# Queue order in the down products and the first attention blocks of a two-layer hybrid trunk: matmul-bound kernel, one core

## The chip, the core and the metric

The kernel runs on one core of a Trainium2 chip. The metric is the time of one execution in microseconds (us) on the device. A core has a matrix engine (TensorE, PE in the profile, with PEld for its weight loads), a vector engine (VectorE, DVE), an activation engine (ScalarE, ACT), a general engine (GpSimd, POOL) and a sync engine (SyncE, SP), which here only issues transfers. Each engine works through its own list of instructions in the order in which they stand there; engines wait for each other through semaphores. Matmuls write to eight PSUM banks, from which VectorE and ScalarE read.

## The reference

Two layers, on 512 tokens of 1024 features in f32. Cut to what matters:

```python
h = rms_norm(x, mix_norm[0])                      # layer 0
q, k, v, cb, cc, cx = split(h @ hy_w_in, ...)     # attention 512+128+128, convolution 3 x 512
attn = sliding_window_attention(rope(norm(q)), rope(norm(k)), v, sinks)   # window 128, blocks of 128
conv = cb * causal_conv3(cc * cx)
x = x + concat(attn, conv) @ hy_w_out
h = rms_norm(x, mix_norm[1])                      # layer 1: chunked gated linear attention
x = x + gla(h, ...) @ gla_w_out
# after the mixer of each layer i
u = causal_conv3(rms_norm(x, ffn_norm[i]) @ w_up[i]) + b[i]     # 1024 -> 2 x 2816
x = x + (gelu(u_gate) * u_up) @ w_down[i]                       # 2816 -> 1024
x = x + sigmoid(rms_norm(x, ple_norm[i]) @ w_gate[i]) * (p[i] @ w_proj[i])
```

## The kernel before

Activations are kept transposed: features on the 128 partitions, the 512 tokens along a row; `xT[0]` to `xT[7]` are the eight rows of x. Every large product is made of three matmuls in a rounded f32 format: each operand is split into a high part (ScalarE rounds it, `activation(h, src, Copy)`) and a low part (VectorE subtracts, `tensor_tensor(l, src, h, subtract)`), and high x high, high x low and low x high are summed in PSUM (`mm3`, lines 166 to 168). So each piece of weights costs one ScalarE and one VectorE instruction before PE may use it: `cut` (lines 146 and 147, tiles `wh` and `wl`), `cut_blocks` (852 and 853) and `split` (109 and 110).

PSUM is held in two pools of four banks, `ps` and `pa`. Weights arrive from memory in `raw` buffers (two), loaded through the SP queue.

Who decides the order. The program is traced top to bottom, and a planner orders each engine's instructions by priority (the order of tracing) and by when they become ready by its own estimate of times. Two things are fixed by hand: inside `manual_schedule(engines=...)` the engines named keep the order of tracing, and `with tc.issue_after(x):` puts every instruction traced in the block on x's own engine behind x in that engine's list. It adds no wait: an instruction of another engine in the block is not touched.

**Layer 0's mixer (`mixer0`).** After keys, values and the four query blocks, PE alternates between the convolution's projections ("x", "c" and "b", each in two pieces `j2` of 256 columns: `conv_in`, 48 matmuls) and the attention of four blocks t of 128 queries: `query_turned(t)` (PE transposes, ScalarE copies to `qT`, line 547), `scores(t)` (PE, line 611; VectorE adds the mask and takes row maxima, 620; then the small steps 627 to 631, the last of which is `es`; ScalarE takes the exponentials, 634), `probs(t)` (scaling, 648 and 652; PE transposes 16 tiles, 658; copies to `pT`, 664 and 666, the latter kept as `copied[t, g]`), and `mix(t)` (675). Each piece of the later convolution weights is cut in two halves, `conv_halves`, whose second half is traced later; their order is tied to copies of the attention. `conv_taps` starts with a ScalarE copy `cxs` (722). `load_vectors1` loads four small vectors through the POOL queue into rows, transposes them on PE (226) and copies them to `vec1` (227). PE's order in this part is the planner's.

**The down projection (`down`).** The product with w_down runs in units u of 256 columns, by a written plan of ordinary pieces (`cut`, 512 columns of tokens) and of block products: eight of the 22 row tiles go through a seven-product scheme on 2 x 2 blocks (`seven`, lines 905 to 907, 256 columns), one such product s for each unit, interleaved with steps of an ordinary piece. For a block product the weights are needed in forms. `first_forms` rounds two blocks as they are, and then makes two differences in place (876 and 877); `cut_blocks(ev)` rounds those (`t13`); `more_forms` makes two more. Inside `seven`, four ScalarE copies carry partial sums from bank to bank (916, 917, 926, and 930, which is `turned_over`). For s = 1 and 3 the weights come in two `zt` buffers (`load_inner`), and first_forms splits two blocks with `split`; for s = 0 and 2 they come in `raw`, and one `cut_blocks` rounds both. At the end of a block product its two sums are added to `xT` by VectorE (`add`, line 1213), which frees their banks for the next one. PE's order here is the traced one, the other engines' is the planner's.

When a row of xT is complete, `finish(m)` prepares it for the next stage: in layer 0 `advance`, in layer 1 `blocks`, which for odd m makes block sums `s12` and `s34` and splits them (`parts`).

Of the kernel before, what the change touches and what calls it, by code (L numbers as in the profile page):

```python
# [14 lines left out]
ALU = mybir.AluOpType  # L15
# [41 lines left out]
class Kernel:  # L57
# [147 lines left out]

        self.nc.gpsimd.tensor_copy(x, self.gate[: x.shape[0]])

    def columns(self, name, views, q=None):

        nc = self.nc  # L210
        n = sum(v.shape[0] for v in views)
        rows = self.sp.tile([P, P], F32, tag="vrow", name=self.nm("vrow"))
        if q is None and self.gate is not None:
            self.late(rows[:, :1])
        at = 0
        for v in views:
            (q or nc.gpsimd).dma_start(rows[at : at + v.shape[0], :], v)
            at += v.shape[0]
        if q:

            nc.scalar.copy(self.few(4, "rs", 4), self.mhalf[:, :4])
        col = self.cp.tile([P, -(-n // 64) * 64], F32, tag=name, name=self.nm(name), bufs=1)[:, :n]

        def finish():
            ps = self.pa()
            nc.tensor.transpose(ps[:, :n], rows[:n, :], self.ident[:n, :n])
            (nc.vector.tensor_copy if q else nc.scalar.copy)(col, ps[:, :n])
            return col

        return finish if q else finish()  # L230

    def load_vectors0(self):
        a = self.a
# [9 lines left out]
    def load_vectors1(self):  # L243
        a = self.a
        f = lambda v: v.rearrange("i (k p) -> (i k) p", p=P)
        v = self.columns(
            "vec1", [f(a["ffn_norm"]), f(a["ple_norm"]), f(a["hy_conv_w"][0]), f(a["gla_o_norm"])]
        )
# [42 lines left out]
    def blocks(self, m, gain, scratch, tags):  # L291


        nc = self.nc
        H = S // 2
        gx = scratch()
        nc.scalar.activation(gx, self.xT[m], AF.Copy, scale=gain[:, m : m + 1])

        def parts(x):
            w = x.shape[1]  # L300
            h, l = self.pair(self.fp, *tags)
            self.halves = self.split((h[:, :w], l[:, :w]), x)
            return lambda b, c: (h[:, b * H + c * P : b * H + (c + 1) * P], l[:, b * H + c * P : b * H + (c + 1) * P])

        if m % 2 == 0:
            self.even = gx
            self.e1 = parts(gx[:, :H])
            self.e1_split = self.halves
        else:
            e, o = self.even, gx  # L310
            op = parts(o)
            s12, s34 = scratch(), scratch()
            nc.vector.tensor_tensor(s12[:, :H], e[:, H:], o[:, H:], ALU.add)
            nc.vector.tensor_tensor(s12[:, H:], s12[:, :H], e[:, :H], ALU.subtract)
            s12p = parts(s12)
            nc.vector.tensor_tensor(s34[:, :H], e[:, :H], e[:, H:], ALU.subtract)
            nc.vector.tensor_tensor(s34[:, H:], o[:, :H], s12[:, H:], ALU.subtract)
            s34p = parts(s34)
            e1 = self.e1
            at = lambda f, b: lambda c: f(b, c)  # L320
            self.forms.append(
                dict(e1=at(e1, 0), o1=at(op, 0), o2=at(op, 1), s1=at(s12p, 0), s2=at(s12p, 1), s3=at(s34p, 0),
                     s4=at(s34p, 1))
            )
        self.squares(m)
# [101 lines left out]
    def mixer0(self):  # L427
        nc, a, tc = self.nc, self.a, self.tc
        with tc.tile_pool(name="m0", bufs=1) as mp:
# [165 lines left out]
            ss, dens, copied, mixed = {}, {}, {}, {}  # L595
            ya = [self.pair(self.fp, "b0", "b1") for _ in range(4)]

            def scores(t):

                w = 2 * P if t else P  # L600
                k0 = (t - 1) * P if t else 0
                mask = self.amask if t else self.amask[:, P:]
                s = mp.tile([P, NQ, 2 * P], F32, tag="s", name=self.nm("s"), bufs=2)
                mx = self.few(8, "mx")
                for h2 in range(2):

                    pbs = [self.pa(), self.pa()]
                    for hh in range(2):
                        hq = 2 * h2 + hh
                        for g in range(2):  # L610
                            nc.tensor.matmul(
                                pbs[g][:, hh * 256 : hh * 256 + w],
                                qTs[t][64 * g : 64 * g + 64, hq, :],
                                kT[64 * g : 64 * g + 64, k0 : k0 + w],
                                start=True, stop=True,
                            )
                    for hh in range(2):
                        for g in range(2):
                            head = 4 * g + 2 * h2 + hh
                            nc.vector.tensor_tensor_reduce(  # L620
                                s[:, head, :w], pbs[g][:, hh * 256 : hh * 256 + w], mask,
                                scale=1.0, scalar=-1e30, op0=ALU.add, op1=ALU.max,
                                accum_out=mx[:, head : head + 1],
                            )

                nm = self.few(8, "nm")
                nc.vector.scalar_tensor_tensor(out=nm, in0=mx, scalar=HD**-0.5, in1=sink, op0=ALU.mult, op1=ALU.max)
                nc.vector.tensor_scalar_mul(nm, nm, -1.0)
                den = self.few(8, "den")
                es = self.few(8, "es")  # L630
                nc.vector.tensor_tensor(es, sink, nm, ALU.add)
                nc.scalar.activation(es, es, AF.Exp)
                for head in range(NQ):
                    nc.scalar.activation(
                        s[:, head, :w], s[:, head, :w], AF.Exp, bias=nm[:, head : head + 1], scale=HD**-0.5,
                        accum_out=den[:, head : head + 1],
                    )
# [58 lines left out]
            def conv_halves(nme, j2, ins):  # L696
# [5 lines left out]
                def half(ins):  # L702
                    c = slice(len(ws) * P, len(ws) * P + P)
                    with tc.issue_after(ins):
                        ws.append(self.cut(raw[:, :, c], "b"))

                half(ins)
                return (lambda k, a, b: ws[a // P](k, 0, P)), half

            def conv_in(nme, w):  # L710
# [6 lines left out]
            def conv_taps(j2):  # L717
                for c in range(2):
                    j = 2 * j2 + c
                    xs = mp.tile([P, S], F32, tag="cxs", name=self.nm("cxs"), bufs=2)  # L720
                    pad = mp.tile([P, S + 2], F32, tag="pad", name=self.nm("pad"), bufs=2)
                    nc.scalar.copy(xs, pss["x", c])
# [19 lines left out]
                    yc[2 * j2 + c] = hl  # L742


            w = conv_w("x", 0)
            R = self.spread()
            qn0 = query(0)
# [1 line left out]
            conv_in("x", w)  # L749
            w = conv_w("c", 0)  # L750
            query_turned(0, qn0)
            self.load_vectors1()
            self.gate = None
            R2 = self.sp.tile([P, S], F32, tag="R", name="R2")
            nc.gpsimd.tensor_tensor(R2, R, R, ALU.mult)
            qn2 = query(2)
            query_turned(1, qn1)
            scores(0)
            conv_in("c", w)
            w, second = conv_halves("b", 0, copied["q", 1])  # L760
            conv_taps(0)
# [3 lines left out]
            second(copied[0, 1])  # L765
            scores(1)
            conv_in("b", w)
            w, second = conv_halves("x", 1, copied[0, 1])
            conv_out(0, (0,))
            query_turned(3, qn3)  # L770
            mix(0)
            probs(1)
            with tc.issue_after(copied[1, 0]):
                conv_out(0, (1,))
            second(mixed[0])
            scores(2)
            conv_in("x", w)
            w, second = conv_halves("c", 1, copied[1, 1])
            second(copied[1, 1])
            mix(1)  # L780
            probs(2)
            scores(3)
            conv_in("c", w)
            w, second = conv_halves("b", 1, copied[2, 1])
            second(copied[2, 1])
            conv_taps(1)
            mix(2)
            probs(3)
# [75 lines left out]
    def first_forms(self, ev, od, raw=None):  # L864
# [5 lines left out]
        else:  # L870
            h, l = self.wide("wh", 16), self.wide("wl", 48)
            h, l = (x.rearrange("p (j u n) -> p j u n", u=2, n=P) for x in (h, l))
            for u, b in enumerate((b11, b21)):
                self.split((h[:, :, u], l[:, :, u]), b)
            plain = lambda j, c: (h[:, j, c], l[:, j, c])
        nc.vector.tensor_tensor(b11, b12, b11, ALU.subtract)
        nc.vector.tensor_tensor(b12, b22, b12, ALU.subtract)  # L877
        return plain

    def more_forms(self, ev, od):  # L880
# [245 lines left out]
    def down(self, i, acts, forms, both, work, finish):  # L1126
# [93 lines left out]
        with tc.manual_schedule(engines={ET.PE}):  # L1220
# [4 lines left out]
            for t, (u, name, k0, k1, s) in enumerate(plan):  # L1225
# [34 lines left out]
                else:  # L1260
# [20 lines left out]
                    if s == 3:  # L1281
                        banks[3] = [X, Y]
                    else:
                        add(2 * s, X)
                        add(2 * s + 1, Y)
                    pend()
                    due[s] -= 1
                    block_left -= 1
# [865 lines left out]
```

## Time and profile before

| what | value |
|---|---|
| median of 3 runs | 1199.35 us (1198.14 to 1199.67) |
| the profiled execution, its own time | 1199.04 us |
| its span, first to last instruction | 1197.2 us |
| instructions | 17966 |
| granted TensorE clock | 1.000 |
| busy: DVE, ACT, POOL | 994.0, 684.0, 42.9 us |
| memory read and written | 114.37 MB and 2.10 MB, 97 GB/s over the span |
| chain that ended last, by engine | PE 89%, DVE 5%, ACT 3%, issue 2%, POOL 1% |

Busy time is the time in which an engine has an instruction on record. The views used are: the page's shares and slices; the waits (who waited for whom); the timeline (instructions in order of time, equal neighbours merged, with the idle time before them and what ended it in brackets); and the groups of instructions by line, with the busy time, the mean duration and the idle time before them. In a row, `wl<-raw,wh` names the tile written and those read, `128x1024` partitions by elements.

### The profile page before, as it was taken

The page shows a single profiled execution, that of the slowest core. Times are in us where ns is not written, and L with a number is a line of the kernel's source. Part 1 is how long each engine was busy: PE and PEld are TensorE (multiplying, and loading weights), DVE is VectorE, ACT ScalarE, POOL GpSimd, SP SyncE. Part 2 cuts the span into 40 slices and gives each one's busy share as a digit, 9 for nine tenths or more (in the row PEclk, how much of TensorE's full clock was granted, in tenths as well). Part 3 has the DMA queues.
Part 4 walks back from the last instruction along what each step waited for, and adds up shares of the span by engine and source line. Part 5 has one row for each costly group of instructions (what it writes and reads, how often), then busy time and mean ns, then how long its engine had stood idle before and what let it go on. Part 6 is the DMA issues. An engine that isn't in the chain of part 4 may idle for free.

```text
span 1197.2 us, 17966 instructions
## 1 busy us (share of the span) xinstructions
PE 1189.6 (99%) x7121; PEld 1039.0 (87%) x7121; DVE 994.0 (83%) x1571; ACT 684.0 (57%) x1116; POOL 42.9 (4%) x64
## 2 busy tenths in 40 slices
PE   9999999999999999999999999999999999999998
PEld 8877789999998888989988988889999999889887
DVE  6777687899999986789779876687999999976895
ACT  7566465655565644566563664555555656643764
POOL 2600000000000000000100000000000000000000
PEclk9999999999999999999999999999999999999999
DMA  7212322424232332232412222323242424323601
GB/s 223 85 58 72 108 71 71 142 71 141 71 122 90 122 126 97 97 106 64 148 59 70 73 70 71 106 67 110 71 141 71 141 71 131 125 89 97 212 1 71
DMA packets 110856, 117.62 MB, mean 98 GB/s; under 512 B 2824, under 2 KB 105794, under 8 KB 110772
## 3 DMA queue, kind: packets, MB, share of 16 engines
q1 hardware_dynamic: 109936, 115.88, 29.9%
q8 instruction: 56, 0.92, 0.3%
q0 software_dynamic: 560, 0.42, 0.3%
q10 hardware_dynamic: 276, 0.18, 0.1%
q14 instruction: 28, 0.23, 0.1%
HBM read 114.37 MB, written 2.10 MB: 97 GB/s over the span
## 4 chain that ended last, share of the span: by engine, by line
PE 89%; DVE 5%; ACT 3%; issue 2%; POOL 1%; DMA 0%; SPq 0%; DVEq 0%; ACTq 0%; POOLq 0%
PE ps L166 12%; PE ps L168 12%; PE ps L167 12%; PE pa L167 7%; PE pa L166 7%; PE pa L168 7%; PE ps L905 6%; PE ps L907 6%; PE ps L906 6%; PE pa L907 2%; PE pa L905 2%; PE pa L906 2%; PE ps L1519 1%; PE ps L1518 1%; PE ps L1517 1%
## 5 line engine op out<-in xcount | busy, mean ns | idle before, releaser
L146 ACT ACTIVATE wh<-raw 128x1024 fp32r<-128x1024 f32 (+4 forms) x144 | 143.4, 999 | 97.0 <-PE ps L167 59.3
L147 DVE TENSOR_TENSOR wl<-raw,wh 128x1024 fp32r<-128x1024 f32 (+4 forms) x144 | 165.7, 1151 | 28.6 <-ACT wh L146 27.7
L852 ACT ACTIVATE wh<-raw 128x1024 fp32r<-128x1024 f32 x84 | 89.3, 1063 | 121.6 <-DVE raw L877 65.4
L965 DVE SCALAR_TENSOR_TENSOR zt<-z,vfa,zt 128x510 f32<-128x510 f32 (+1 forms) x176 | 130.6, 744 | 5.3 <-ACT zt L963 4.7
L853 DVE TENSOR_TENSOR wl<-raw,wh 128x1024 fp32r<-128x1024 f32 x84 | 102.6, 1221 | 20.6 <-ACT wh L852 20.5
L963 ACT ACTIVATE zt<-z,vfb 128x512 f32<-128x512 f32 x88 | 71.0, 809 | 20.8 <-DVE four L1016 8.3
L166 PE MATMUL ps<-b,wh 128*128 128x512 f32 x192 | 76.2, 397 | 0.0
L167 PE MATMUL ps<-b,wh 128*128 128x512 f32 x192 | 75.0, 391 | 0.0
L168 PE MATMUL ps<-b,wl 128*128 128x512 f32 x192 | 74.9, 390 | 0.0
L905 PE MATMUL ps<-four,wh 128*128 128x256 f32 x256 | 71.6, 280 | 0.0
L907 PE MATMUL ps<-four,wl 128*128 128x256 f32 x256 | 71.1, 278 | 0.0
L906 PE MATMUL ps<-four,wh 128*128 128x256 f32 x256 | 70.9, 277 | 0.0
L167 PE MATMUL pa<-b,wh 128*128 128x512 f32 x176 | 69.0, 392 | 0.0
L167 PE MATMUL pa<-a,wh 128*128 128x512 f32 x176 | 69.0, 392 | 0.0
L166 PE MATMUL pa<-a,wh 128*128 128x512 f32 x176 | 69.0, 392 | 0.0
L166 PE MATMUL pa<-b,wh 128*128 128x512 f32 x176 | 69.0, 392 | 0.0
L168 PE MATMUL pa<-b,wl 128*128 128x512 f32 x176 | 68.4, 389 | 0.0
L168 PE MATMUL pa<-a,wl 128*128 128x512 f32 x176 | 68.4, 389 | 0.0
L166 PE MATMUL ps<-a,wh 128*128 128x512 f32 x128 | 50.6, 395 | 0.0
L167 PE MATMUL ps<-ul,wh 128*128 128x512 f32 x128 | 50.1, 391 | 0.0
L166 PE MATMUL ps<-uh,wh 128*128 128x512 f32 x128 | 50.1, 391 | 0.0
L167 PE MATMUL ps<-a,wh 128*128 128x512 f32 x128 | 50.0, 390 | 0.0
(496 smaller groups left out, 3591.3 us busy)
## 6 DMA issues: line engine op xcount, KB each, us to landing
raw<-in_ffn_w_up_dram SPq DMA_DIRECT2D x44, 1024.0 KB, 5.1
raw<-in_ffn_w_down_dram SPq DMA_DIRECT2D x12, 1024.0 KB, 5.2
raw<-in_hy_w_in_dram SPq DMA_DIRECT2D x8, 1024.0 KB, 5.1
raw<-in_gla_w_in_dram SPq DMA_DIRECT2D x8, 1024.0 KB, 5.1
raw<-in_ffn_w_down_dram SPq DMA_DIRECT2D x8, 768.0 KB, 4.5
raw<-in_ple_w_gate_dram SPq DMA_DIRECT2D x6, 1024.0 KB, 5.3
raw<-in_hy_w_out_dram SPq DMA_DIRECT2D x16, 256.0 KB, 4.0
zt<-in_ffn_w_down_dram SPq DMA_DIRECT2D x8, 512.0 KB, 3.6
```

The source lines that it names most:

```text
L146: nc.scalar.activation(hv, v, AF.Copy)
L147: self.rest = nc.vector.tensor_tensor(lv, v, hv.bitcast(F32), ALU.subtract)
L166: mm(out, lh, rh, start=start, stop=False, **kw)
L167: mm(out, lh, rl, start=False, stop=False, **kw)
L168: return mm(out, ll, rh, start=False, stop=stop, **kw)
L852: nc.scalar.activation(h, src, AF.Copy)
L853: nc.vector.tensor_tensor(l, src, h.bitcast(F32), ALU.subtract)
L905: mm(out, wh, xh, start=first and j == 0, stop=False, **kw)
L906: mm(out, wh, xl, start=False, stop=False, **kw)
L907: mm(out, wl, xh, start=False, stop=j == ND // 2 - 1, **kw)
L963: nc.scalar.activation(y, z, AF.Identity, scale=w2[:, f : f + 1], bias=bb[:, f : f + 1])
L965: nc.vector.scalar_tensor_tensor(out=y[:, tap:], in0=z[:, : S - tap], scalar=w[:, f : f + 1], in1=y[:, tap:], op0=ALU.mult, op1=ALU.add,)
```

## The change

Four places. (1) In the down projection `first_forms` splits the second of its two blocks after the two differences instead of before them, on VectorE behind the second difference, and the two adds of a block product to `xT` stand on VectorE behind the second difference of the next product. (2) In layer 1, for rows 0 and 1, ScalarE's rounding of s12 stands behind `turned_over`. (3) The halves of the convolution weights "x", "c" and "b" of piece 1 get further bounds: VectorE's part behind `es` of the scores then running (`begun`), and ScalarE's part of the second half of "x" behind the second `pT` copy of block 1. (4) `load_vectors1` loads earlier in the tracing and transposes after `scores(0)`; ScalarE's `cxs` copies of piece 0 stand behind the copy of query block 1.

```diff
-    def columns(self, name, views, q=None):
+    def columns(self, name, views, q=None, later=False):
...
-        return finish if q else finish()
+        return finish if q or later else finish()
...
     def load_vectors1(self):
...
+        views = [f(a["ffn_norm"]), f(a["ple_norm"]), f(a["hy_conv_w"][0]), f(a["gla_o_norm"])]
+        finish = self.columns("vec1", views, later=True)
+        def turned():
+            self.take_vectors1(finish())
+        return turned
...
     (blocks)
-            s12p = parts(s12)
+            with ExitStack() as es:
+                if m == 1:
+                    es.enter_context(self.tc.issue_after(self.turned_over.ins))
+                s12p = parts(s12)
...
     (scores)
-                nc.vector.tensor_tensor(es, sink, nm, ALU.add)
+                begun[t] = nc.vector.tensor_tensor(es, sink, nm, ALU.add).ins
...
     (conv_halves: half takes several instructions, one issue_after for each)
...
     (conv_taps)
-                    nc.scalar.copy(xs, pss["x", c])
+                    with ExitStack() as es:
+                        if not j2:
+                            es.enter_context(tc.issue_after(copied["q", 1]))
+                        nc.scalar.copy(xs, pss["x", c])
...
     (the order of mixer0)
+            vectors1 = self.load_vectors1()
             w = conv_w("x", 0)
...
             query_turned(0, qn0)
-            self.load_vectors1()
...
             scores(0)
+            vectors1()
             conv_in("c", w)
...
-            w, second = conv_halves("x", 1, copied[0, 1])
+            w, second = conv_halves("x", 1, copied[0, 1], begun[1])
...
-            second(mixed[0])
+            second(mixed[0], copied[1, 1])
...
-            w, second = conv_halves("c", 1, copied[1, 1])
-            second(copied[1, 1])
+            w, second = conv_halves("c", 1, copied[1, 1], begun[2])
+            second(copied[1, 1], begun[2])
...
-            w, second = conv_halves("b", 1, copied[2, 1])
-            second(copied[2, 1])
+            w, second = conv_halves("b", 1, copied[2, 1], begun[3])
+            second(copied[2, 1], begun[3])
...
     (first_forms)
-            for u, b in enumerate((b11, b21)):
-                self.split((h[:, :, u], l[:, :, u]), b)
+            self.split((h[:, :, 0], l[:, :, 0]), b11)
             plain = lambda j, c: (h[:, j, c], l[:, j, c])
         nc.vector.tensor_tensor(b11, b12, b11, ALU.subtract)
-        nc.vector.tensor_tensor(b12, b22, b12, ALU.subtract)
+        self.differed = nc.vector.tensor_tensor(b12, b22, b12, ALU.subtract)
+        if raw is None:
+            with self.tc.issue_after(self.differed.ins):
+                self.split((h[:, :, 1], l[:, :, 1]), b21)
...
     (down)
-                        add(2 * s, X)
-                        add(2 * s + 1, Y)
+                        with tc.issue_after(self.differed.ins):
+                            add(2 * s, X)
+                            add(2 * s + 1, Y)
```

More of the change, by code (lines that the diff above doesn't have):

```diff
@@ L245, in load_vectors1, with take_vectors1 @@
         f = lambda v: v.rearrange("i (k p) -> (i k) p", p=P)
-        v = self.columns(
-            "vec1", [f(a["ffn_norm"]), f(a["ple_norm"]), f(a["hy_conv_w"][0]), f(a["gla_o_norm"])]
-        )
+        views = [f(a["ffn_norm"]), f(a["ple_norm"]), f(a["hy_conv_w"][0]), f(a["gla_o_norm"])]
[3 more added lines that the diff above has]
+        return turned
+    def take_vectors1(self, v):
         self.g_ffn = [v[:, i * 8 : 8 + i * 8] for i in range(2)]
@@ L593, in query_turned @@
                 qTs.append(qT)
-            ss, dens, copied, mixed = {}, {}, {}, {}
+            ss, dens, copied, mixed, begun = {}, {}, {}, {}, {}
             ya = [self.pair(self.fp, "b0", "b1") for _ in range(4)]
@@ L694, in conv_w, with conv_halves @@
                 return self.weights(w_in[:, :, c0 : c0 + 256], ND, 256)
[L696 removed]
+            def conv_halves(nme, j2, *ins):
                 c0 = starts[nme] + 256 * j2
@@ L700, in conv_halves, with half @@
                 ws = []
-                def half(ins):
+                def half(*ins):
                     c = slice(len(ws) * P, len(ws) * P + P)
-                    with tc.issue_after(ins):
+                    with ExitStack() as es:
+                        for x in ins:
+                            es.enter_context(tc.issue_after(x))
                         ws.append(self.cut(raw[:, :, c], "b"))
-                half(ins)
+                half(*ins)
                 return (lambda k, a, b: ws[a // P](k, 0, P)), half
@@ L721, in conv_taps @@
                     pad = mp.tile([P, S + 2], F32, tag="pad", name=self.nm("pad"), bufs=2)
-                    nc.scalar.copy(xs, pss["x", c])
+                    with ExitStack() as es:
+                        if not j2:
+                            es.enter_context(tc.issue_after(copied["q", 1]))
+                        nc.scalar.copy(xs, pss["x", c])
                     nc.gpsimd.memset(pad[:, :2], 0.0)
```

## The prediction

> **What bounds the kernel now.** The page comes first: engine shares and the slices of the granted clock.
>
> ```profile
> PE 1189.6 (99%) x7121; PEld 1039.0 (87%) x7121; DVE 994.0 (83%) x1571; ACT 684.0 (57%) x1116; POOL 42.9 (4%) x64
> ```
>
> ```profile
> PEclk9999999999999999999999999999999999999999
> ```
>
> The kernel is bound by TensorE (PE), at its full granted clock from end to end. No matmul is added or removed here, so the edit can only close or open gaps in PE's stream, and 99% leaves room for little.
>
> Next the waits of PE, of which this is the longest, and PE's rows in time where that wait falls, in the down projection of layer 0 (the first two columns are start and duration in us, then engine, line, what is written and read):
>
> ```profile
> PE pa L907 <- DVE wl L853: 1.2, 4, 0.7
> ```
>
> ```profile
> 457.60 0.28 PE L905 MATMUL pa<-a,wh 128*128 128x256 f32 x1
> 457.72 0.28 PE L906 MATMUL pa<-a,wh 128*128 128x256 f32 x1
> 458.68 0.39 PE L907 MATMUL pa<-a,wl 128*128 128x256 f32 x1 [0.68 <-DVE wl L853]
> 458.90 0.28 PE L905 MATMUL pa<-a,wh 128*128 128x256 f32 x1
> ```
>
> L907 starts 0.96 after L906, where 0.12 is usual (457.60 to 457.72), and the one behind it comes 0.22 later instead of 0.12. So this wait costs 0.84 + 0.10 = 0.94 us, not the 0.68 in brackets. The other places where the same kind of row shows a gap (layer 0, then three in layer 1):
>
> ```profile
> 473.95 0.28 PE L906 MATMUL pa<-a,wh 128*128 128x256 f32 x1
> 474.40 0.39 PE L907 MATMUL pa<-a,wl 128*128 128x256 f32 x1 [0.17 <-DVE wl L853]
> ```
>
> ```profile
> 1074.12 0.28 PE L906 MATMUL pa<-b,wh 128*128 128x256 f32 x1
> 1074.61 0.39 PE L907 MATMUL pa<-b,wl 128*128 128x256 f32 x1 [0.20 <-DVE wl L853]
> ```
>
> ```profile
> 1089.88 0.28 PE L906 MATMUL pa<-b,wh 128*128 128x256 f32 x1
> 1090.33 0.39 PE L907 MATMUL pa<-b,wl 128*128 128x256 f32 x1 [0.17 <-DVE wl L853]
> ```
>
> ```profile
> 1113.15 0.39 PE L167 MATMUL ps<-four,wh 128*128 128x512 f32 x1
> 1113.38 0.39 PE L168 MATMUL ps<-four,wl 128*128 128x512 f32 x1
> 1113.98 0.38 PE L905 MATMUL ps<-b,wh 128*128 128x256 f32 x1 [0.21 <-ACT ps L930]
> ```
>
> How little is open has to be read from such starts, not from busy time, for the record of a matmul is longer than the spacing of two: of 256 columns they start 0.12 us apart (457.60 to 457.72) and are booked with 0.28, of 512 columns 0.23 apart (1113.15 to 1113.38) and booked with 0.39. A gap under about 0.16 us never shows as idle. With these spacings and 0.10 for the restart the four places cost 0.43, 0.47, 0.43 and 0.60 - 0.23 + 0.10 = 0.47.
>
> By the Trainium skill, page "Perfetto Trace Analysis", section "Identifying the Most-Contended Engine", matmul busy time is a poor measure of headroom and the busy share of the weight loads the better one; by it 13% of the span would be open here, an estimate of 156 us. The starts disagree: the same 87% stands beside a stream without gaps, and the measurement decides.
>
> **The change, part by part.**
>
> *The weight halves of the block products* (first_forms and the two adds behind differed). What L907 waited for at 458.68 is this, on DVE and then ACT:
>
> ```profile
> 452.65 1.28 DVE L110 TENSOR_TENSOR wl<-zt,wh 128x512 fp32r<-128x512 f32 x2
> ```
>
> ```profile
> 454.46 0.68 DVE L1213 TENSOR_TENSOR xT<-xT,ps 128x512 f32<-128x512 f32 x1
> 455.05 0.68 DVE L877 TENSOR_TENSOR zt<-zt,zt 128x512 f32<-128x512 f32 x1
> ```
>
> ```profile
> 457.40 1.22 DVE L853 TENSOR_TENSOR wl<-zt,wh 128x1024 fp32r<-128x1024 f32 x1 [1.06 <-ACT wh L852]
> ```
>
> ```profile
> 456.32 1.04 ACT L852 ACTIVATE wh<-zt 128x1024 fp32r<-128x1024 f32 x1
> ```
>
> L877 makes the differences that ACT's L852 rounds and DVE's L853 subtracts. Ahead of it stand the second of the two L110 (0.60 in the queue) and one add to xT (0.59, 454.46 to 455.05); both now go behind it. So L877 ends at 455.73 - 1.19 = 454.5. L852 is then ready before any xT row is finished, so the work on xT that ACT ran ahead of it (it started at 456.32, 0.6 after L877's end) no longer precedes it: about 454.6 to 455.6. L853 ends at 456.9, or 457.5 if both adds go first; PE wants it at 457.72 + 0.12 = 457.84. The stall goes, with 0.3 to 0.9 to spare. The second L110's product is wanted only with the next product, at 459.97:
>
> ```profile
> 459.97 0.28 PE L905 MATMUL ps<-four,wh 128*128 128x256 f32 x1
> ```
>
> The same queue at 474.40, where both adds stand ahead of L877 and cost 0.59 each:
>
> ```profile
> 470.66 0.68 DVE L1213 TENSOR_TENSOR xT<-xT,ps 128x512 f32<-128x512 f32 x1
> ```
>
> ```profile
> 473.12 1.22 DVE L853 TENSOR_TENSOR wl<-raw,wh 128x1024 fp32r<-128x1024 f32 x1 [1.19 <-ACT wh L852]
> ```
>
> L853 moves from 473.12 to about 471.9 and ends at 473.2; PE wants it at 474.07. The two places in layer 1 are the same code. Gain: 0.94 + 0.43 + 0.47 + 0.43 = 2.27. What is delayed are the adds, by one or two DVE instructions; behind them wait the two PSUM banks that the next block's first copies (L916, L917) fill. The first bank is wanted by PE at 459.97, so 1.2 us of delay from 455.1 is covered. If the cover went, see the rivals.
>
> *Layer 1, s12p behind turned_over.* The copy that PE waited for at 1113.98, L930, stood behind other work on ACT:
>
> ```profile
> 1112.21 1.45 ACT L109 ACTIVATE b<-zt 128x256 fp32r<-128x256 f32 x3
> 1113.56 0.36 ACT L930 COPY ps<-ps 128x256 f32<-128x256 f32 x1
> ```
>
> Three roundings of blocks stand ahead. The last is s12p's, 512 wide, about 0.5 of the 1.45; without it L930 starts near 1113.05 and ends at 1113.4, before the 1113.61 at which PE gets there. Gain 0.47. s12p itself is not read before the down projection has ended.
>
> *Second attention block.* PE's 16 transpositions of probs(1), and the same 16 of probs(2) undisturbed:
>
> ```profile
> 84.83 1.98 PE L658 MATMUL pa<-cf,s 128*128 128x128 f32 x12
> 87.02 0.66 PE L658 MATMUL pa<-cf,s 128*128 128x128 f32 x4 [0.22 <-ACT qT L547]
> 87.66 0.48 PE L611 MATMUL pa<-kT,qT 64*128 64x256 f32 x1
> ```
>
> ```profile
> 103.04 1.97 PE L658 MATMUL pa<-cf,s 128*128 128x128 f32 x16
> ```
>
> 2.83 from 84.83 to 87.66, against 1.97: 0.86 lost. Two causes stand in the queues of DVE and ACT:
>
> ```profile
> 77.62 1.22 DVE L147 TENSOR_TENSOR wl<-raw,wh 128x1024 fp32r<-128x1024 f32 x1
> ```
>
> ```profile
> 85.45 1.05 ACT L146 ACTIVATE wh<-raw 128x1024 fp32r<-128x1024 f32 x1
> 86.40 0.57 ACT L547 COPY qT<-pa 128x512 f32<-128x512 f32 x1
> ```
>
> L147 is the first half of "x" 1; it holds the row maxima, hence all exponentials and the scaling of block 1, up by some 1.1 of its 1.22. Behind begun[1] it no longer does. L146 is the second half; it holds up the copy of query 3, which frees the bank for the last four transpositions, by 0.95. Behind copied[1, 1] it no longer does. Both halves serve a projection that begins after scores(2), so after 87.66, and its second half 24 matmuls (24 x 0.23 = 5.5) later; 1.05 + 1.22 after the copies of block 1 fits. Gain 0.86. The same edges on "c" 1 and "b" 1 move only DVE's half, by three instructions on 8 columns, in stretches where PE has no gap: nothing.
>
> *First scores.*
>
> ```profile
> 55.98 0.26 PE L226 MATMUL pa<-cf,vrow 46*128 46x46 f32 x1
> 56.17 0.66 PE L546 MATMUL pa<-cf,qn 128*128 128x128 f32 x4
> 56.58 0.47 PE L166 MATMUL ps<-a,wh 128*128 128x512 f32 x1
> 56.98 1.23 PE L611 MATMUL pa<-kT,qT 64*128 64x128 f32 x16
> ```
>
> ```profile
> 55.77 0.57 ACT L722 COPY cxs<-ps 128x512 f32<-128x512 f32 x1
> ```
>
> L226, the norm vectors' transposition, takes 0.19 (55.98 to 56.17); it leaves this place and is paid a little later, so it is worth nothing by itself. L611 starts 0.40 after L166 instead of 0.23, held by query copies behind L722 on ACT; with L722 behind both copies, that 0.17 goes. I take 0.2, between -0.1 (L226 alone in a stream of projections costs a restart) and +0.3 (its own restart here goes as well). The four loads of the vectors and their gate are only traced earlier on POOL, which is busy 4%; the later load that reuses their buffer waits for L226 and now issues later, with the whole attention still ahead of its use. SP gets no new instruction: a buffer of raw weights is freed up to about 1 us later by the delayed halves.
>
> Sum: 2.27 + 0.47 + 0.86 + 0.2 = 3.8 us. The profiled execution took 1199.04 (span 1197.2), 0.31 under the median 1199.35; so 1195.2 for a run like it and 1195.5 for the median.
>
> **Rivals.** (a) Only the projections gain: DVE and ACT stay as crowded before probs(1), since all orders there come from a planner. 2.27 + 0.47 = 2.74: 1196.6. For it: 84.83 has two causes, and both must go.
>
> (b) L226 lands behind the first scores and PE stands. By then all four "pa" banks belong to scores(0), and the first comes free with the third L620 on DVE:
>
> ```profile
> 61.57 0.28 DVE L620 CUSTOM_DVE_ANT_0 s<-pa,cf 128x128 f32<-128x128 f32 x1
> ```
>
> PE would stand from 58.2 (the end of L611 above) to 61.9, less what projection matmuls the planner puts between: 3.5, in all 1195.5 + 3.5 = 1199.0. Against it: in the rows above a projection matmul (56.58) fills the wait for the query's copy, so L226, ready early, should fill that slot, with a bank still free. A stand that long could also cost pace. The first matmuls of the kernel, on a PE just started, are slower than the 0.23 of later ones of their size:
>
> ```profile
> L202 PE MATMUL pa<-ones_r 128*128 128x512 f32 x10 | 4.3, 586 | 1.3 <-DVE mhalf L190 1.3
> ```
>
> That is 0.43 apiece; ten such after the stand would lose 10 x 0.20 = 2.0 more: 1201.0, of (b)'s chance I give it 0.02. By the Trainium skill, page "TensorE: Matmul & The Clock Gate", section "HAM oscillation — how this bites in real kernels", an idle gap of more than about 3.4 us brings the halved clock back. No gap of this trace is so long, so no row tests it.
>
> (c) Slower: the adds slip too far. If they queue behind L884, L887 and the t2 split instead of beside L853, the first ends at 456.9 + 3 x 0.68 + 0.6 = 459.6, its copy L916 at 459.9, and PE wants the bank at 459.97 - 0.94 = 459.0: 0.9 and a restart of 0.1 at each of six hand-overs (three per layer), 6.0 in all; 1201.5. It turns the sign once it costs over 0.6 each, that is, once the first add ends after 459.2. Against it: the adds are traced ahead of those steps.
>
> (d) The edges change no order that matters: 1199.35.
>
> **Numbers.** Main 0.60, (a) 0.14, (b) 0.11, (c) 0.10, (d) 0.05. The range runs from 1194.6 (main with +0.3 at the scores, the missing tail of 0.1, and 0.5 between runs) to 1199.2, so that (a) and (b) are inside; left out are (c) and (d). About 0.2%, 2.4 us, is what a measurement here can tell from no change: faster is main, most of (a), less some loss on each for parts that come half: 0.63; within it most of (b), (d) and those halves: 0.26; slower (c) and the little of (b) that loses pace: 0.11.
>
> **What would show it.** PE's waits on wl L853 vanish, L907 follows L906 by 0.12 at all four places, L905 follows L168 by 0.23 at the fifth; the 16 transpositions of probs(1) take 1.9; L226 stands between the queries' transpositions and L611. Wrong: L226 with a wait on DVE L620 behind it, a wait of L905 on ACT L916 or L917, or new gaps in PE's starts between 90 and 135.

## The result: 1200.8 us instead of 1195.5, a little slower than before

Over 20 runs the changed kernel has a median of 1200.79 us (1199.70 to 1203.80), the kernel before 1199.20 (1198.14 to 1200.13, 20 runs): a ratio of 1.0015, interval 1.0009 to 1.0022. The forecast was 1195.5, in a range from 1194.6 to 1199.2. The profiled execution took 1199.70, with a span of 1197.8; it is the shortest of the 20. The changed kernel's lines are shifted: 546 and 547 are now 555 and 556, 611 is 620, 620 is 629, 658 is 667, 675 is 684, 722 is 736, 852 and 853 are 867 and 868, 877 is 891, 905 to 907 are 922 to 924, 916, 917 and 930 are 933, 934 and 947, 1213 is 1230.

The page looks as before, and its 40 slices of 30 us show nothing:

```profile
PE 1188.1 (99%) x7121; PEld 1039.6 (87%) x7121; DVE 994.7 (83%) x1571; ACT 685.3 (57%) x1116; POOL 43.0 (4%) x64
```

The waits of PE tell the story in one line (engine, tile and line that waited, what it waited for, us in all, times, longest). Those of before on wl L853, ps L930 and qT L547 are gone, and this one is new:

```profile
PE pa L226 <- DVE mx L629: 4.0, 1, 4.0
```

PE in order of time, where it falls:

```profile
55.23 1.03 PE L555 MATMUL pa<-cf,qn 128*128 128x128 f32 x8
56.02 0.47 PE L166 MATMUL ps<-a,wh 128*128 128x512 f32 x1
56.51 1.20 PE L620 MATMUL pa<-kT,qT 64*128 64x128 f32 x16
61.73 0.34 PE L226 MATMUL pa<-cf,vrow 46*128 46x46 f32 x1 [4.02 <-DVE mx L629]
61.99 0.80 PE L167 MATMUL ps<-a,wh 128*128 128x512 f32 x1
62.59 0.63 PE L168 MATMUL ps<-a,wl 128*128 128x512 f32 x1
63.01 0.63 PE L166 MATMUL ps<-a,wh 128*128 128x512 f32 x1
...
65.00 0.39 PE L168 MATMUL ps<-a,wl 128*128 128x512 f32 x1
65.23 0.40 PE L166 MATMUL ps<-a,wh 128*128 128x512 f32 x1
```

The norm vectors' transposition L226 is no longer between the queries' transpositions and the scores; it stands behind the scores, and PE stands still with it (below, the stand) from 57.6, the scores' end at the pace of before, to 61.73. Behind it the projection starts its matmuls 0.43 apart (62.59 to 63.01) instead of 0.23 (65.00 to 65.23): PE has lost pace. This is rival (b), with its loss of pace, and the sign that the prediction had named for being wrong. What L226 waits for, on DVE:

```profile
59.47 1.57 DVE L593 TENSOR_TENSOR qn<-m,rq 128x256 f32<-128x256 f32 x4
60.96 0.28 DVE L629 CUSTOM_DVE_ANT_0 s<-pa,cf 128x128 f32<-128x128 f32 x1
...
61.38 0.29 DVE L629 CUSTOM_DVE_ANT_0 s<-pa,cf 128x128 f32<-128x128 f32 x1
```

DVE works on queries 2 and 3 until 61, and then reduces the scores. The third reduction, which ends at 61.67, is the last reader of the first of the four banks of scores(0); L226 starts 0.06 later. So it waited for that bank, the first of the four to come free. PE had other work meanwhile: in other_bank, below, the projection's matmuls follow the scores at once. That none of them was put ahead of L226 is the planner's order, and no run shows why it chose it.

The granted clock there, in stretches of 1 us (the number ahead of the DMA share, third from the end, is PEclk):

```profile
60.00:61.00 1.00, 0.00 (x0) 0.00 (x0) 0.94 (x4) 0.00 (x0) 0.25 (x1) 1.00 1.08 381
61.00:62.00 1.00, 0.27 (x2) 0.19 (x2) 1.00 (x10) 0.00 (x0) 0.00 (x0) 0.71 0.28 95
62.00:63.00 1.00, 1.00 (x3) 0.82 (x3) 1.00 (x9) 0.88 (x2) 0.64 (x2) 0.50 0.00 0
...
64.00:65.00 1.00, 1.00 (x4) 0.77 (x3) 0.32 (x2) 0.82 (x5) 0.00 (x0) 0.59 0.17 39
```

0.71 over 61 to 62 is 0.58 us at half speed, so the clock fell at 61.42; 0.59 over 64 to 65 is 0.82 at half speed, so it came back at 64.82. So it was halved for 3.40 us, in 3.1 of which PE was at work.

Both kernels then reach the same place, the output projection, the first rows being of before and the second of the changed kernel, and so do the last matmuls:

```profile
134.68 0.48 PE L166 MATMUL ps<-b,wh 128*128 128x512 f32 x1
```

```profile
138.48 0.48 PE L166 MATMUL ps<-b,wh 128*128 128x512 f32 x1
```

```profile
1192.66 0.28 PE L1519 MATMUL ps<-four,a 128*128 128x256 f32 x1
```

```profile
1193.21 0.28 PE L1537 MATMUL ps<-four,a 128*128 128x256 f32 x1
```

3.80 behind at 138.48, 0.55 behind at the end: the rest of the kernel, in which only parts (1) and (2) of the change lie, gained 3.25 us. The five gaps of the down projections, in the changed kernel (before: 0.96, 0.45, 0.49, 0.45 and 0.60 apart), the first and the last shown; the three between are 0.12:

```profile
461.53 0.28 PE L923 MATMUL pa<-a,wh 128*128 128x256 f32 x1
461.64 0.28 PE L924 MATMUL pa<-a,wl 128*128 128x256 f32 x1
...
1114.46 0.39 PE L168 MATMUL ps<-four,wl 128*128 128x512 f32 x1
1114.68 0.28 PE L922 MATMUL ps<-b,wh 128*128 128x256 f32 x1
```

and the second attention block, whose 16 transpositions took 2.83 before, first the projection behind its scores in the kernel before, then the changed kernel:

```profile
90.04 0.50 PE L166 MATMUL ps<-a,wh 128*128 128x512 f32 x1
```

```profile
90.04 1.97 PE L667 MATMUL pa<-cf,s 128*128 128x128 f32 x16
91.94 2.00 PE L620 MATMUL pa<-kT,qT 64*128 64x256 f32 x16
93.86 0.50 PE L166 MATMUL ps<-a,wh 128*128 128x512 f32 x1
```

1.90 from 90.04 to 91.94, as forecast. The scores behind them close up as well: 1.92 to the next projection, against 2.38 before (87.66, in the prediction's rows, to 90.04).

### The profile page after: what moved, and what is told of

Read it like the earlier page. It is cut to its first block, busy times and chain, and to the rows that moved or that the text cites. A ratio compares the mean times of both kernels' runs of the same rounds, so it can differ in the third digit from the quotient of the medians.

```text
span 1197.8 us, 17965 instructions
## 1 busy us (share of the span) xinstructions
PE 1188.1 (99%) x7121; PEld 1039.6 (87%) x7121; DVE 994.7 (83%) x1571; ACT 685.3 (57%) x1116; POOL 43.0 (4%) x64
## 4 chain that ended last, share of the span: by engine, by line
PE 96%; DVE 1%; issue 1%; POOL 1%; ACT 1%; POOLq 0%; ACTq 0%
PE ps L166 13%; PE ps L167 13%; PE ps L168 13%; PE pa L167 7%; PE pa L166 7%; PE pa L168 7%; PE ps L922 6%; PE ps L924 6%; PE ps L923 6%; PE pa L922 2%; PE pa L924 2%; PE pa L923 2%; PE ps L1537 1%; PE ps L1536 1%; PE ps L1535 1%
## 5 line engine op out<-in xcount | busy, mean ns | idle before, releaser
L868 DVE TENSOR_TENSOR wl<-raw,wh 128x1024 fp32r<-128x1024 f32 x84 | 102.8, 1224 | 20.9 <-ACT wh L867 20.9
L168 PE MATMUL ps<-a,wl 128*128 128x512 f32 x128 | 50.3, 393 | 0.0
```

The costliest lines, as they stand in the source:

```text
L168: return mm(out, ll, rh, start=False, stop=stop, **kw)
L868: nc.vector.tensor_tensor(l, src, h.bitcast(F32), ALU.subtract)
```

## The experiments

### Is it the bank, the place or the data?

The theory: `pa` hands out its four banks in turn, in the order in which they are asked for. The call traced behind scores(0) is the one behind that block's four requests, and so gets that block's first bank, whatever else may be free when L226 runs. Three kernels change only which request is made, or when. **other_bank** takes the bank from the other pool:

```diff
         def finish():
-            ps = self.pa()
+            ps = self.ps() if later else self.pa()
```

> The changed kernel, with one word altered: the norm vectors' transposition L226 writes a bank of the ps pool instead of one of the pa pool. It is still traced behind scores(0). Theory A (the stand of 4.1 us is a wait for the pa bank that the rotation hands out fifth, the first of scores(0)'s four): L226 runs between the queries' transpositions and the first scores, no wait on DVE L629 is left, no matmul runs at half pace, and the time is that of before, 1199.2, less what the other parts brought in the trace of the changed kernel (3.27 in the down projections, 1.35 in the second attention block, 0.3 at the first scores): 1194.3. Rival B (L226 waits for its rows, which come late, or for its place behind the scores): the stand stays, 1200.8.

Measured: 1194.62 us (ratio to before 0.9963, 0.9950 to 0.9975). PE's order differs from the changed kernel's by this one transposition:

```profile
55.73 1.03 PE L555 MATMUL pa<-cf,qn 128*128 128x128 f32 x8
56.70 0.26 PE L226 MATMUL ps<-cf,vrow 46*128 46x46 f32 x1
...
57.31 1.16 PE L620 MATMUL pa<-kT,qT 64*128 64x128 f32 x16
58.40 0.50 PE L167 MATMUL ps<-a,wh 128*128 128x512 f32 x1
58.73 0.39 PE L168 MATMUL ps<-a,wl 128*128 128x512 f32 x1
```

L226 stands where the forecast wanted it, no wait on DVE L629 is left, and the pace behind is full from 58.73 on. So its rows are there in time and its place in the tracing is no obstacle: rival B is out.

**before_scores** keeps the `pa` pool and moves the call up by one line:

```diff
             query_turned(1, qn1)
+            vectors1()
             scores(0)
-            vectors1()
```

> The changed kernel, with the call that turns the norm vectors moved up by one line: behind query 1's transposition and ahead of scores(0), still in a bank of the pa pool. Theory A (what counts is which request takes which bank: the fifth behind four of one block waits for that block): L226 gets the bank ahead of the scores', runs in the slot before them as with the other bank, and the time is 1194.5. If the pa pool itself is the trouble, whatever the order of the requests, PE stands again somewhere before 62: 1198 or more.

Measured: 1194.75 us (0.9966, 0.9954 to 0.9978). L226 runs in the same slot, ahead of the scores:

```profile
56.16 0.26 PE L226 MATMUL pa<-cf,vrow 46*128 46x46 f32 x1
...
56.77 1.16 PE L620 MATMUL pa<-kT,qT 64*128 64x128 f32 x16
```

With other_bank this shows that it is neither the pool nor the place of the call, but the order of the requests: they are served in the order of the tracing, whatever the order in which the instructions could run. Whether the four banks go round in turn, as the theory has it, or the planner hands out the one that it expects free first, the runs do not tell apart, for the first bank of scores(0) is both.

**old_place** turns the vectors where the kernel before does, with the rest of the change kept:

```diff
             query_turned(0, qn0)
+            vectors1()
             self.gate = None
...
             scores(0)
-            vectors1()
```

> The changed kernel, with the norm vectors turned where the kernel before turns them, between the two queries' transpositions; their loads still start earlier, and the convolution's first copies still stand behind the queries. Theory A: 1194.3, as with the other bank, perhaps 0.1 more, since L226 stands between query 0 and query 1 and delays the latter by 0.19. Rival C (the earlier loads or the copies behind the queries are what costs): still above 1199.

Measured: 1194.40 us (0.9958, 0.9945 to 0.9972). Rival C is out. The profiles of old_place and other_bank each have one wait on ACT L947 in a later product (0.7 and 0.4 us), that of before_scores has none; its cause is open. These three are all some 4.5 us faster than before and 6 faster than the changed kernel, and cannot be told apart by their 5 or 6 runs each.

### The parts alone

**vectors_only**: the kernel before, with only these lines of the change and what they need in `columns` and `load_vectors1`:

```diff
+            vectors1 = self.load_vectors1()
             w = conv_w("x", 0)
...
-            self.load_vectors1()
...
             scores(0)
+            vectors1()
```

> The kernel before with one part of the change alone: the norm vectors' loads start ahead of the convolution's first weights, and their transposition is traced behind scores(0). Theory A: L226 stands about 4.1 us behind the scores with a wait on the reductions (L620 of the kernel before), and the matmuls behind it run at half pace for 1.3 to 3.5 us of loss; L226's old place (0.2) is saved: 1199.2 + 4.1 + 1.3 to 3.5 = 1204.6 to 1206.8, likeliest 1205.5. Rival C (the stand needs the other parts of the change, such as the copies behind the queries): below 1201.

Measured: 1204.63 us (1.0048, 1.0033 to 1.0062), 5.58 above the 1199.05 of before beside it and at the lower end of what was expected. In its profile (lines 3 lower than in the changed kernel) the stand is there without the other parts, so rival C is out here too, and ten matmuls are slow, not six:

```profile
56.79 1.20 PE L617 MATMUL pa<-kT,qT 64*128 64x128 f32 x16 [0.18 <-ACT qT L553]
61.84 0.33 PE L226 MATMUL pa<-cf,vrow 46*128 46x46 f32 x1 [3.85 <-DVE mx L626]
...
62.69 0.63 PE L168 MATMUL ps<-a,wl 128*128 128x512 f32 x1
...
66.11 0.63 PE L167 MATMUL ps<-a,wh 128*128 128x512 f32 x1
```

**down_only**: the kernel before with parts (1) and (2) of the change, cut:

```diff
+        if raw is None:
+            with self.tc.issue_after(self.differed.ins):
+                self.split((h[:, :, 1], l[:, :, 1]), b21)
...
+                        with tc.issue_after(self.differed.ins):
                             add(2 * s, X)
                             add(2 * s + 1, Y)
...
+                    es.enter_context(self.tc.issue_after(self.turned_over.ins))
                 s12p = parts(s12)
```

> The kernel before with the down products' part alone: the second weight half and the two adds behind the differences, and in layer 1 the blocks of s12 behind the turned rows. The forecast's term: -2.74, 1196.5. The trace of the changed kernel counted from before, matmul by matmul: -3.27, since three hand-overs that the forecast did not count (0.15 to 0.21 each) closed as well: 1195.9. No stand and full pace all through.

Measured: 1196.23 us (0.9979, 0.9970 to 0.9988), 2.82 below before, between the two expectations. The waits on wl L853 and ps L930 are gone, and no new one of that kind has come.

**halves_only**: the kernel before with part (3), cut:

```diff
+            w, second = conv_halves("x", 1, copied[0, 1], begun[1])
...
+            second(mixed[0], copied[1, 1])
...
+            w, second = conv_halves("c", 1, copied[1, 1], begun[2])
...
+            w, second = conv_halves("b", 1, copied[2, 1], begun[3])
```

> The kernel before with the attention's part alone: the halves of x 1, c 1 and b 1 behind begun[1], copied[1, 1], begun[2] and begun[3]. The forecast's term: -0.86, 1198.3. The trace of the changed kernel counted from before: -1.35, since the second scores close up by 0.45 as well: 1197.85. If the gain came from the later start of block 1 (everything in the changed kernel reaches it 5.2 us later) and not from these edges: 1199.2.

Measured: 1197.96 us (0.9988, 0.9980 to 0.9997), 1.09 below before. Block 1 is reached at the old time here (84.82, before 84.83), and its transpositions still close up, so the edges do it and not a later start:

```profile
84.82 1.97 PE L658 MATMUL pa<-cf,s 128*128 128x128 f32 x16
86.72 2.04 PE L611 MATMUL pa<-kT,qT 64*128 64x256 f32 x16
88.69 0.50 PE L166 MATMUL ps<-a,wh 128*128 128x512 f32 x1
```

-2.82, -1.09 and +5.58 add up to +1.67; the whole change measures +1.59. Each of these medians can be some tenths off, so that they agree so closely says little.

**old_place_no_copies**: old_place without the edge on the `cxs` copies.

```diff
-                        if not j2:
-                            es.enter_context(tc.issue_after(copied["q", 1]))
                         nc.scalar.copy(xs, pss["x", c])
```

> The kernel old_place (all of the change, with the norm vectors turned between the queries), less the edge that puts the convolution's first two copies behind query 1's. The forecast's term: the scores start 0.17 later, 1194.4 + 0.2 = 1194.6. In old_place itself the slot between the projection's matmul and the scores is still 0.40 wide, as in the kernel before, so the edge may bring nothing: 1194.4.

Measured: 1195.19 us (0.9967, 0.9956 to 0.9979). In both profiles the scores follow the projection's matmul by 0.40, with the edge (the order fixed by `issue_after`) and without it. In old_place the copy of query block 0, the only one that scores(0) reads, had no `cxs` copy ahead of it and was over at 56.32:

```profile
55.73 0.59 ACT L556 COPY qT<-pa 128x512 f32<-128x512 f32 x1 [0.22 <-PE pa L555]
```

```profile
56.22 0.47 PE L166 MATMUL ps<-a,wh 128*128 128x512 f32 x1
56.62 1.23 PE L620 MATMUL pa<-kT,qT 64*128 64x128 f32 x16
```

The scores started 0.30 after that all the same. So the 0.17 that the forecast took for a wait on this copy was none, as long as L226 stands between the queries. Without L226 there the edge does act: the slot is 0.49 in the changed kernel (56.02 to 56.51) and 0.66 in vectors_only, which lacks the edge, with a wait on the copy of 0.18 in the row above.

The 0.8 between the medians of five and six runs does not come from this place. The profiled executions stand the other way round (1195.28 and 1194.98), and their traces differ elsewhere: the wait for the first weights (on ACT L112) is 0.7 in old_place and 1.2 here, and the one wait on L947 costs old_place 1.0 with its restart. From the projection behind the first scores (57.78 and 58.70; before 58.14) to the last matmul (1188.82 and 1188.62; before 1192.66) old_place gains 3.5 on the kernel before, 4.5 but for that wait, and this kernel 4.6. So in these two traces the edge is worth nothing.

### What the stand costs, and what idling costs

Matmuls that nobody reads are put ahead of L226, into a `ps` bank of their own. They leave the stand as long as it is and take idle time out of it. **fill16**, and with 8 and 4 in place of 16 **fill8** and **fill4** (written over more lines here than in the kernel; `rhs` is `ones_r` spread over 512 columns):

```diff
         def finish():
+            busy = later and self.ps()
+            for _ in range(16 * later):
+                nc.tensor.matmul(busy, self.ones_r, rhs, start=True, stop=True)
             ps = self.pa()
```

> The changed kernel, with 16 matmuls of 512 columns into an otherwise unused ps bank ahead of L226; nothing reads them. One takes the slot before the first scores, 15 stand behind the scores and fill 15 x 0.227 = 3.4 of the 4.1 us that PE stands, so that 0.7 is left idle. Theory A with a pace loss that comes from idling: the stand costs its 4.1 as before, no matmul after it runs slow, one projection matmul (0.23) is displaced: 1194.3 + 4.1 + 0.3 = 1198.7, about 2 below the changed kernel's 1200.8, though PE has 16 matmuls more to do, and a narrower spread. Rival D (the slow matmuls after the stand come from something else, such as ACT and DVE reading the banks): the pace loss stays, 1200.8 to 1201.0, and the pitch of 0.43 is seen again.

> The same with 8 such matmuls: 7 behind the scores fill 1.6 us, so that PE idles for about 2.5 us instead of 4.1. If the pace is lost only by an idle time above some length between 2.5 and 4.1: 1198.7, as with 16. If it is lost in proportion to the idle time: about 0.6 of the 2.1 stay, 1200.0. If any idle of this size costs it whole: 1200.8.

> The changed kernel with 4 matmuls of 512 columns ahead of L226, as in fill16 and fill8: 3 behind the scores leave PE idle for 3.4 of the 4.1 us. In fill8 (2.4 idle) the profiled execution kept its pace, and 3 of 11 runs had a mean clock of 0.998 and some 1.3 us more than the others; in the changed kernel (4.1 idle) the profiled execution lost 1.3 us and the runs have 0.995 to 0.999. If the loss comes by chance, the more often the longer the idle time (the clock judged at moments that have no tie to the kernel): half or more of the runs lose 1 to 2, median 1199.5 to 1200.5. If there is a sharp length above 3.4: 1199.0. If below: 1200.8, every run slow.

The idle time in the table is that of the profiled execution, by starts: the row's, and the 0.16 by which a record is longer than the spacing.

| kernel | idle in the stand, us | median | runs, spread | ratio to before | runs with a mean clock of 0.998 or less |
|---|---|---|---|---|---|
| fill16 | 0.5 | 1198.80 | 11, 1197.95 to 1201.16 | 0.9996 (0.9987 to 1.0004) | 0 |
| fill8 | 2.4 | 1199.01 | 11, 1198.06 to 1200.76 | 1.0001 (0.9992 to 1.0010) | 3 |
| fill4 | 3.3 | 1200.54 | 11, 1198.77 to 1201.95 | 1.0012 (1.0003 to 1.0020) | 4 |
| the change | 4.1 | 1200.79 | 20, 1199.70 to 1203.80 | 1.0015 (1.0009 to 1.0022) | 15 |

In the profile of fill16 the stand is as long as in the changed kernel (57.60 to 61.67), and the pace behind it is whole:

```profile
57.60 3.69 PE L225 MATMUL ps<-ones_r 128*128 128x512 f32 x15
61.67 0.26 PE L226 MATMUL pa<-cf,vrow 46*128 46x46 f32 x1 [0.38 <-DVE mx L629]
...
62.20 0.40 PE L167 MATMUL ps<-a,wh 128*128 128x512 f32 x1
62.44 0.40 PE L168 MATMUL ps<-a,wl 128*128 128x512 f32 x1
```

In that of fill8 PE idles for 2.4 (2.20 by the row), and there too the pace is whole in the profiled execution:

```profile
61.28 0.26 PE L226 MATMUL pa<-cf,vrow 46*128 46x46 f32 x1 [2.20 <-DVE mx L629]
```

So fill16's PE has 16 matmuls more to do and the kernel is 2.0 faster: the slow matmuls come from idling, and rival D is out. Of the 6.2 between the changed kernel and other_bank (1194.62), 4.2 are the stand (1198.80 - 1194.62, a displaced matmul of 0.23 among them) and 2.0 the pace (1200.79 - 1198.80).

The last column counts the executions whose clock was halved for longer than the 3.40 us of the changed kernel's profile (3.4 us at half speed are 1.7 of 1198, a mean of 0.9986, which is printed as 0.999, as it is for some runs of the kernel before). It is no measure of the time lost, for a halved stretch costs nothing where PE stands: a mean of 0.996 goes with 1200.15 and with 1202.12 in the changed kernel. The column rises with the idle time, and so do the medians, but one kernel's runs do not all lose the same: of fill8's 11 runs six lie from 1198.06 to 1199.01 and five from 1200.01 to 1200.76; of fill4's one is at 1198.77 and ten from 1199.93 up. That fits the expectation of a loss by chance, the more often the longer the idle time; the difference between fill8 and fill4 in the last column (3 and 4 of 11) is too small to show it alone. fill16's longest run, 1201.16 at a clock of 0.999, is not explained by it.

The clock itself: in fill4's profile it is halved from 61.80 to 65.20, in the changed kernel's from 61.42 to 64.82: 3.40 us both. In vectors_only:

```profile
59.00:60.00 1.00, 0.00 (x0) 0.00 (x0) 1.00 (x3) 0.00 (x0) 1.00 (x1) 0.92 1.04 364
60.00:61.00 1.00, 0.00 (x0) 0.00 (x0) 0.94 (x3) 0.00 (x0) 0.35 (x1) 0.50 1.08 386
...
66.00:67.00 1.00, 1.00 (x4) 0.76 (x4) 0.00 (x0) 1.00 (x6) 0.00 (x0) 0.67 0.00 0
```

from 59.84 (0.92 is 0.16 at half) to 66.66 (0.67 is 0.66 at half): 6.8, twice as long. The Trainium skill, page "TensorE: Matmul & The Clock Gate", section "What's actually happening", says that activity is judged over free-running windows of about 3.4 us; these stretches agree. The same section lowers the clock after an idle window; here it fell 1.9 us after PE had stopped, with PE at work for the scores (56.79 to 57.9, 1.1 us) and little more in the 3.4 us before. So the clock can fall before PE has been idle for a whole window, and the measurement decides. In the changed kernel it fell 3.8 us after the stop (57.6 to 61.42) and in fill4 3.2 (58.6 to 61.80): no fixed time of standing explains all three.

## Why the prediction was wrong, point by point

**The step that failed** is the term "First scores", taken as a gain of 0.2, and in it above all one clause, "so L226, ready early, should fill that slot, with a bank still free". The slot and the readiness were right, and so was the planner's choice where a bank is to be had, as other_bank and before_scores show. The bank was wrong. I had counted four `pa` banks as four that any instruction may take when it runs; the bank is given out before the kernel runs, in the order of the tracing, and moving the call behind scores(0) moved its request behind four others. Alone (vectors_only) this part loses 5.58.

The gain in the same term was wrong as well. That the scores start late because they are "held by query copies behind L722 on ACT" does not hold: in old_place the copy has no L736 (L722 before) ahead of it and the slot stays 0.40. With the bank put right the term is nothing: from the first transposition of queries to the projection behind the scores it is 2.67 in other_bank (55.73 to 58.40) and 2.69 in old_place (55.09 to 57.78), and before it was 55.45 to 58.14, or 2.69.

**Rival (b)** named place, waiter and releaser, and got 0.11. Its price, 3.5, was low: it took off something for projection matmuls that the planner would put between, and there were none, and the scores now end at 57.6 and not at 58.2; the stand is 4.1. Its loss of pace, 2.0 for ten matmuls, was right in size (2.0 in the median, six to ten matmuls in the profiles), and wrong in chance: I gave it 0.02 of 0.11, where it came in the profile of the shortest run and, by the clock, for longer still in 15 of 20 runs. That its sum, 1201.0, lies so near the 1200.8 measured is partly luck: without L226's stand the kernel takes 1194.6 (other_bank) and not 1195.5, and the stand with its pace costs 6.2 and not 5.5.

**The down products** were forecast at 2.74 and measured 2.82 alone. The five gaps closed as said, and the queue was right too: one of the two adds went ahead of L868, the other behind it. Layer 0, in the changed kernel:

```profile
457.90 0.69 DVE L891 TENSOR_TENSOR zt<-zt,zt 128x512 f32<-128x512 f32 x1
...
459.12 0.68 DVE L1230 TENSOR_TENSOR xT<-xT,ps 128x512 f32<-128x512 f32 x1
459.79 1.23 DVE L868 TENSOR_TENSOR wl<-zt,wh 128x1024 fp32r<-128x1024 f32 x1
460.93 0.68 DVE L1230 TENSOR_TENSOR xT<-xT,ps 128x512 f32<-128x512 f32 x1
```

L868 ends at 461.0, PE wants it at 461.64: 0.6 to spare, within the 0.3 to 0.9 forecast. Rival (c), adds that slip, did not come: PE waits for no L933 or L934. In its trace the changed kernel gains 3.25 in these products, 0.5 more than the five gaps, from small hand-overs that I had not counted; the 2.82 of the median lies between the two. Rival (a) is out by halves_only.

**The attention halves** were forecast at 0.86 and measured 1.09 alone. The trace of halves_only gives 0.93 to the transpositions (2.83 to 1.90 by starts; I had taken the 1.97 of a record) and 0.41 more to the scores behind them (2.38 to 1.97), which I had not looked at.

Forecast without the failed term: 1199.2 - 2.74 - 0.86 = 1195.6. Measured with the term put right: 1194.4 to 1194.75. What these two terms missed makes the difference: by the traces they bring 3.25 + 1.34 = 4.6, and 1199.2 - 4.6 = 1194.6. The medians of the parts alone give less, 3.9 together; their runs lie up to 2.7 us apart, and no run shows more of it. One sum in the prediction is off as well: the lower end of the range, 1194.6, goes down from the profiled run's 1195.2; from the forecast for the median, 1195.5, it would be 1194.8.

## What to carry to other kernels

When a step that takes a buffer from a rotating pool is moved in the tracing, move the request in your mind first: count how many requests of the pool lie between it and the one whose buffer it will get, and who frees that. Ready data and an open slot help nothing if the buffer is bound to a late reader; taking it from another pool or asking one line earlier was worth 6 us here. Nor is the engine sure to do other ready work meanwhile: in its list that work may stand behind. A stand of a matmul-bound engine costs more than its length: in these runs 4.2 us of standing cost 2.0 more in pace.

## What the runs showed of the hardware

In the three profiles that show a halved clock behind the stand it lasted 3.40, 3.40 and 6.8 us, and it began 3.8, 3.2 and 1.9 us after PE had stopped. Whether it comes, and for how long, differs between executions of one kernel: a mean clock of 0.998 or less stands beside none of 11 runs at 0.5 us of idle time, three of 11 at 2.4, four of 11 at 3.3, 15 of 20 at 4.1. Feeding PE matmuls that nobody reads in a wait that is there anyway gave back 2.0 of the 6.2 us. The clock on record does not show every slow stretch: in the kernel before, matmuls of L202 start 0.43 apart from 1.9 to 4.5 us, and the granted clock stands at 1.00 there.
